# The router's column sums behind the first half of the output projection, the residual's factor on VectorE, the further blocks' slots two pairs later

## Chip, cores and metric

One core of one Trainium2 chip. The metric is device time in microseconds (us) of one execution of the program; lower is better.

## What is computed

One layer of a decoder for 512 tokens of width 1024, all in float32: a token mixer (attention, pooling and a state-space branch, merged and projected by `w_out`), a norm, a mixture of 32 experts, and a norm. What the change touches is the end of the first part and the start of the second. Cut from the reference:

```python
x = layer_norm(DN_ALPHA * x + mix, ln1_g, ln1_b)          # mix = merged @ w_out
p_grp = softmax(xf @ w_grp + b_grp); g_sel = argmax(p_grp)
logit_e = (xf @ w_exp + b_exp)                            # top 2 experts inside the group
h = silu(xb @ w_gate[e]) * (xb @ w_up[e]); y = h @ w_down[e]
x = layer_norm(DN_ALPHA * x + ffn, ln2_g, ln2_b)          # DN_ALPHA = 2 ** 0.25
```

## The kernel before

**Front part.** `out_proj` multiplies the merged activations (`mh`, `ml`: a high and a low part) by `w_out` (`whl`: the same split). Each product takes three matmuls (L70, L71, L72). The first 512 columns of `w_out` are done for all four tiles of 128 tokens at once: 4 chunks of `whl` x 2 row blocks x 4 tiles x 3 = 96 matmuls into banks `ps_mm` and `ps_s`. Then, tile by tile, the second 512 columns follow, with the transposes of the finished rows (L1055), the router's logits (L1065) and the norm. The norm's gain is folded into the router's weights by `router_consts`: it loads the weights `wr` on ScalarE's DMA queue, multiplies them on VectorE (L933, L934), adds them up per column (`wsum`, L936), spreads the sums over all partitions by one matmul against ones (L938), and reads the result into `nsg` and `br` (L940, L941), which only the logits need (L1068, L1069).

**Expert part.** `moe` takes the experts in pairs. A pair's token rows are gathered from DRAM by an indirect DMA on POOL's queue (`fetch`, L1335), transposed (L1342) and multiplied by an expert's gate and up weights (64 matmuls, L1355); `hidden` makes `th` on ScalarE and VectorE; `turn` transposes it (L1374) and ScalarE copies it to `hT` (L1375); `flush` runs the 16 down matmuls (L1387), whose bank `ps_o` ScalarE and VectorE empty into `y` (L1391, L1393). After each pair `combine` adds the rows into `acc` (L1408, L1409 on TensorE, L1418 on VectorE). All expert weights, 192 pieces of 1 MB, come through SP's DMA queue in one fixed order into a ring of buffers (L1439); a piece is issued when the buffer that it goes into has been read.

**Extras in the first pairs.** `residual(t, c)` loads a half of the first norm's gain and shift into `t` (L1088, on ScalarE's DMA queue), multiplies it by ALPHA on ScalarE (L1089), and applies it to `acc` by 8 VectorE operations (L1092, L1093); it is called at experts 1 and 2. `route_further` (VectorE only) works out where tokens go whose expert has more than 64 rows; `slots_everywhere` (8 transposes of `dd`, L1304, copied to `db`) and `further_slots` (per token tile and choice three VectorE operations that write `og` and `rwo`, L1321 to L1323, and a small matmul, L1324) turn it into tables. All of it stood at experts 1 and 2.

**The loop for further blocks.** Between pairs 7 and 8 stands a loop on the chip (L1558) with a count that is read from memory; for this input its body is not run. All five engines meet at its entry. Ahead of it SP has issued 13 pieces that only experts 16 to 18 need (`held`); the next piece is issued behind the loop. In the compiled order SP's branch into the loop carries waits on the completion of the loads that it has issued; the other engines' branches wait for the release of the common barrier.

Within an engine instructions run in the order of the compiled list; a scheduler makes that list, except where `keep_in_program_order` or `inorder` pins an instruction.

Of the kernel before, what the change touches and what calls it, by code (L numbers as in the profile page):

```python
# [8 lines left out]
F32 = mybir.dt.float32  # L9
# [5 lines left out]
OP = mybir.AluOpType  # L15
# [6 lines left out]
NT = 4  # L22
# [8 lines left out]
ALPHA = 2.0 ** 0.25  # L31
# [8 lines left out]
def dram(ap, offset, dims):  # L40
    return bass.AP(tensor=ap.tensor, offset=ap.offset + offset, ap=dims)


class Build:
# [869 lines left out]
    def router_consts(self, p):  # L914

        nc, I = self.nc, self.I
        V = nc.vector.tensor_tensor
        wr = p.tile([128, KD, 36], F32, name="wr")
        for i in range(2):
            ks = slice(i * 4, i * 4 + 4)  # L920
            nc.scalar.dma_start(wr[:, ks, 0:4], dram(I["router_w_grp"], i * 2048, [[16, 128], [4, 4], [1, 4]]))
            nc.scalar.dma_start(wr[:, ks, 4:36], dram(I["router_w_exp"], i * 16384, [[128, 128], [32, 4], [1, 32]]))
        br = p.tile([128, 36], F32, name="br")
        nc.scalar.dma_start(br[:, 0:4], dram(I["router_b_grp"], 0, [[0, 128], [1, 4]]))
        nc.scalar.dma_start(br[:, 4:36], dram(I["router_b_exp"], 0, [[0, 128], [1, 32]]))
        for i, nm in enumerate(("ln1_g", "ln1_b")):
            nc.scalar.dma_start(self.gb[:, i].rearrange("p (i k) -> p i k", i=2), dram(I[nm], 0, [[4, 128], [512, 2], [1, 4]]))
        ones = p.tile([128, KD, 128], F32, name="xT", bufs=2)[:, 0]
        nc.gpsimd.memset(ones, 1.0)
        bc = [128, KD, 36]  # L930
        wb = p.tile([128, KD, 128], F32, name="xT", bufs=2)[:, :, 0:36]
        sm = p.tile([128, 2, 36], F32, name="wsum")
        V(wb, wr, self.gb[:, 1, :, None].to_broadcast(bc), OP.mult)  # L933
        V(wr, wr, self.gb[:, 0, :, None].to_broadcast(bc), OP.mult)  # L934
        for i, t in enumerate((wr, wb)):
            nc.vector.tensor_reduce(sm[:, i], t.rearrange("p k n -> p n k"), axis=AX.X, op=OP.add)  # L936
        ps = self.bank("o")
        nc.tensor.matmul(ps[:, 0:72], ones, sm.rearrange("p i n -> p (i n)"), start=True, stop=True)  # L938
        nsg = p.tile([128, 36], F32, name="nsg")
        nc.vector.tensor_scalar(nsg, ps[:, 0:36], -1.0, None, op0=OP.mult)  # L940
        V(br, br, ps[:, 36:72], OP.add)  # L941
        return wr, nsg, br

    def out_proj(self, mh, ml):

        nc = self.nc
# [3 lines left out]
        for tt in range(NT):  # L950
# [2 lines left out]
            R.append(r)  # L953
        w = [[self.load_cols(I["w_out"], D, i * 512, 512, k0=4 * j, nk=4, t=self.rc.tile([128, 2048], F32, name="rc", bufs=4))
              for j in range(2)] for i in range(2)]
        rc = self.router_consts(p)

        def evac(half, tt, a):
            o = R[tt][:, half * 512:(half + 1) * 512]
            nc.vector.scalar_tensor_tensor(o, o, 2.0 * ALPHA, a, op0=OP.mult, op1=OP.add)  # L960
# [11 lines left out]
                 for k4 in range(4)]  # L972
        for tt in range(NT):
            evac(0, tt, accs[tt])

        rows = [self.bank("s") for _ in range(2)]
        lg = p.tile([128, NT, 36], F32, name="lg")
# [94 lines left out]
    def norm1_apply(self, p, tt, mv, rs):  # L1072
# [7 lines left out]
            nc.scalar.activation(r[:, c], r[:, c], AF.Identity, bias=nm, scale=rs)  # L1080
        nc.gpsimd.dma_start(self.zd[tt * 128:(tt + 1) * 128], r)

    def residual(self, t, c):

        nc = self.nc
        cs = slice(c * 512, (c + 1) * 512)
        for i, nm in enumerate(("ln1_g", "ln1_b")):
            nc.scalar.dma_start(t[:, i], dram(self.I[nm], c * 512, [[0, 128], [1, 512]]))  # L1088
        nc.scalar.mul(t, t, ALPHA)  # L1089
        for tt in range(NT):  # L1090
            r = self.acc[tt // 2][:, tt % 2, cs]
            self.tc.keep_in_program_order(nc.vector.tensor_tensor(r, r, t[:, 0], OP.mult))  # L1092
            nc.vector.tensor_tensor(r, r, t[:, 1], OP.add)  # L1093


    def first_max(self, p, v, rev, m, oh, name):
# [212 lines left out]
    def further_slots(self, part):  # L1309

        nc = self.nc
        T = nc.vector.tensor_scalar
        p = self.rt
        if part == 0:
            self.fps = self.bank("pt")[0:64, 0:32]
        for tt in (part * 2, part * 2 + 1):
            for i in range(2):
                rk = self.og0[:, tt % 2 * 2 + i, 0:64]
                wo = p.tile([128, 2, 16], F32, name="rwo", bufs=4)
                io, bk = self.io128[:, 0:16], self.blk[:, tt, i:i + 1]  # L1320
                T(rk, self.io64[:, 0:64], self.rr[:, tt, i:i + 1], None, op0=OP.is_equal)  # L1321
                T(wo[:, 0], io, bk, self.tok[:, tt:tt + 1], op0=OP.is_equal, op1=OP.mult)
                T(wo[:, 1], io, bk, self.wk[:, i, tt:tt + 1], op0=OP.is_equal, op1=OP.mult)  # L1323
                self.inorder(nc.tensor.matmul(self.fps, rk, wo.rearrange("p a n -> p (a n)"), start=(tt == 0 and i == 0),  # L1324
                                              stop=(tt == NT - 1 and i == 1)))
        if part:
            T(self.idxo, self.fps[:, 0:16], 4096.0, None, op0=OP.add)
            for h in range(2):
                T(self.wt48[h * 64:(h + 1) * 64, 32:48], self.fps[:, 16:32], 0.5, None, op0=OP.mult)


    def gather(self, xs, idx):
# [119 lines left out]
    def moe(self):  # L1452
        p = self.ep
        self.worder, self.wt = [], []
        for e in range(E + 1):
            gu = [(e, m, i) for m in (0, 1) for i in (0, 1)] if e < E else []
            dn = [(e - 1, 2, i) for i in (0, 1)] if e else []
            self.worder += dn + gu if e == 2 * LOOP else gu + dn
        spare = self.spare
        xs1, gb = spare[:, :D], spare[:, D:].rearrange("p (i n) -> p i n", i=2)  # L1460
        xq = self.xq0
        xs = self.xq0.rearrange("p k n -> p (k n)")
        self.db = p.tile([128, 2, S], I16, name="db")
        pairs = E // 2
        pend = None
        self.terms = []

        def fetch(j, xs=xs):
            if j < pairs:
                self.gather(xs, self.idx[:, j:j + 1])  # L1470

        for e in range(E):
            pr, odd = e // 2, e % 2
            if pr == LOOP and not odd:
                self.flush(pend, self.turn(pend[1]))
                self.combine()
                pend = None

                held = self.worder.index((e, 0, 0)) + len(self.ring) - 7
                self.load_until(held)  # L1480
                self.overflow()
                self.npiece = held
                xq = self.gather_turn(xs)
                fetch(pr + 1)
            hT = []
            gu = self.gate_up(xq[:, :, odd * 64:(odd + 1) * 64], self.pieces(e, 0), self.pieces(e, 1),
                              (lambda: hT.append(self.turn(pend[1]))) if pend and e > 1 else None)
            if e == 0:
                self.load_until(len(self.first))
                fetch(1, xs1)  # L1490
                self.slot_weights()
                pend = (0, self.hidden(gu, self.wt48[:, 0:1]), None)
                continue
            if e == 1:
                fetch(2)
                hT.append(self.turn(pend[1]))
            if e == 2:
                self.slots_everywhere()
                self.further_slots(0)
                pend = (*pend[:2], self.slot_rows(self.sid[:, 0:1]))  # L1500
            end = pr == pairs - 1
            if end and not odd:
                self.load_until(len(self.worder))
            th = self.hidden(gu, self.wt48[:, e:e + 1])
            if odd:
                if not end and pr + 1 != LOOP:

                    xq = self.gather_turn(xs if pr else xs1)
                    if pr:
                        fetch(pr + 2)  # L1510
                if self.terms:
                    self.combine()
                self.y = self.ytile(end)
            if pend:
                self.flush(pend, hT[0])
            if e == 1:
                srt = self.route_further()
            if e == 2:
                self.further_slots(1)
                srt.close()  # L1520
            if e in (1, 2):
                self.residual(gb, e - 1)
            if odd and pr:
                ot = self.slot_rows(self.sid[:, pr:pr + 1], t=self.moe_tile() if end else None)
            pend = (e, th, ot if odd and pr else None)
        self.ahead = [self.start_tile(tt) for tt in range(2)]
        self.flush(pend, self.turn(pend[1]))
        self.steady = False
        return self.terms
# [230 lines left out]
```

## Time and profile before

| | |
|---|---|
| median of 3 runs | 1097.99 us (1094.75 to 1098.54) |
| the profiled execution | 1097.79 us, of which 1096.1 us span from the first to the last instruction |
| mean granted TensorE clock | 0.962 of 2.4 GHz |
| busy time over the span | PE 999.9 us (91%), DVE 593.6 us (54%), ACT 317.0 us (29%), POOL 201.1 us (18%) |
| read from HBM | 254.40 MB, 236 GB/s over the span |

PE is TensorE, DVE VectorE, ACT ScalarE, POOL GpSimd, SP the engine whose queue issues the large loads; a q behind a name is that engine's sequencer or DMA queue. A time is counted from the span's start. Busy shares are means over stages with different limits, so the rows below are read stage by stage. Ends of matmuls are modelled: back-to-back matmuls overlap in the rows, and the distance of their starts is the pace.

### The profile page before, as it was taken

The page shows a single profiled execution, that of the slowest core. Times are in us where ns is not written, and L with a number is a line of the kernel's source. Part 1 is how long each engine was busy: PE and PEld are TensorE (multiplying, and loading weights), DVE is VectorE, ACT ScalarE, POOL GpSimd, SP SyncE. Part 2 cuts the span into 40 slices and gives each one's busy share as a digit, 9 for nine tenths or more (in the row PEclk, how much of TensorE's full clock was granted, in tenths as well). Part 3 has the DMA queues.
Part 4 walks back from the last instruction along what each step waited for, and adds up shares of the span by engine and source line. Part 5 has one row for each costly group of instructions (what it writes and reads, how often), then busy time and mean ns, then how long its engine had stood idle before and what let it go on. Part 6 is the DMA issues. An engine that isn't in the chain of part 4 may idle for free. (4 is left out here: it accounts for less than half of the span.)

```text
span 1096.1 us, 15867 instructions
## 1 busy us (share of the span) xinstructions
PE 999.9 (91%) x6189; PEld 698.7 (64%) x6189; DVE 593.6 (54%) x1427; ACT 317.0 (29%) x662; POOL 201.1 (18%) x179
## 2 busy tenths in 40 slices
PE   7969988999989999999698879999996999999994
PEld 6956676778778777888585455555552655555552
DVE  7992667474788784253255384444444244444436
ACT  4322222334556564232122121111110111111112
POOL 5410213334111223453112000000000000000003
PEclk9995999999999899999899989999998899999997
DMA  6701442225111112735415999999998999999992
GB/s 201 225 1 23 98 82 77 78 71 165 38 39 40 39 39 66 281 115 198 158 74 215 409 382 418 418 418 419 418 419 360 403 418 418 418 418 418 419 375 77
DMA packets 79821, 256.21 MB, mean 234 GB/s; under 512 B 16544, under 2 KB 43712, under 8 KB 55168
## 3 DMA queue, kind: packets, MB, share of 16 engines
q1 hardware_dynamic: 68064, 245.56, 57.4%
q10 hardware_dynamic: 8944, 3.59, 2.1%
q0 software_dynamic: 2736, 6.03, 1.5%
q8 instruction: 49, 0.80, 0.3%
q14 instruction: 28, 0.23, 0.1%
HBM read 254.40 MB, written 4.69 MB: 236 GB/s over the span
## 5 line engine op out<-in xcount | busy, mean ns | idle before, releaser
L1355 PE MATMUL ps_mm<-w,xq 128*64 128x256 f32 x1296 | 148.3, 381 | 0.0
L102 POOL TENSOR_TENSOR whl<-w,whl 128x1024 fp32r<-128x1024 f32 (+3 forms) x41 | 94.7, 2318 | 278.7 <-ACT whl L113 237.9
L1355 PEld LDWEIGHTS ps_mm<-w,xq 128*64 128x64 f32 x1296 | 91.2, 137 | 53.3 <-issue 8.6
L72 PE MATMUL ps_mm<-xh,whl 128*128 128x512 f32 x288 | 115.8, 402 | 0.0
L71 PE MATMUL ps_mm<-xl,whl 128*128 128x512 f32 x288 | 115.4, 401 | 0.0
L70 PE MATMUL ps_mm<-xh,whl 128*128 128x512 f32 x288 | 115.2, 400 | 0.0
L1365 DVE SCALAR_TENSOR_TENSOR th<-th,ps_mm 128x256 f32<-128x256 f32 x32 | 13.5, 421 | 161.2 <-ACT th L1364 161.2
L1393 DVE TENSOR_TENSOR y<-ps_o,y 64x512 fp32r<-64x512 f32 x60 | 41.3, 689 | 86.7 <-ACT y L1391 79.3
L1335 POOL DMA_INDIRECT xq<-zd,idx x14 | 14.0, 1003 | 389.8 <-PE ps_pt L1408 306.3
L1391 ACT CAST y<-ps_o 64x512 fp32r<-64x512 f32 x60 | 34.8, 579 | 141.7 <-issue 81.9
L1387 PE MATMUL ps_o<-w,hT 128*64 128x512 f32 x288 | 69.6, 608 | 0.0
L72 PEld LDWEIGHTS ps_mm<-xh,whl 128*128 128x128 f32 x288 | 54.7, 190 | 11.0 <-issue 0.8
L71 PEld LDWEIGHTS ps_mm<-xl,whl 128*128 128x128 f32 x288 | 54.8, 190 | 10.3
L70 PEld LDWEIGHTS ps_mm<-xh,whl 128*128 128x128 f32 x288 | 54.6, 189 | 10.4 <-issue 0.9
L113 ACT CAST whl<-w 128x1024 fp32r<-128x1024 f32 (+3 forms) x56 | 54.7, 989 | 13.5 <-PE ps_mm L72 13.4
L1355 PE MATMUL ps_mm<-rc,xq 128*64 128x256 f32 x384 | 46.8, 393 | 0.0
L1387 PEld LDWEIGHTS ps_o<-w,hT 128*64 128x64 f32 x288 | 21.4, 139 | 36.0 <-issue 33.0
L1364 ACT ACTIVATE th<-ps_mm 128x256 f32<-128x256 f32 x32 | 12.3, 383 | 104.8 <-PE ps_mm L1355 104.8
L1355 PE MATMUL ps_mm<-rd,xq 128*64 128x256 f32 x368 | 42.2, 381 | 0.0
L1355 PEld LDWEIGHTS ps_mm<-rc,xq 128*64 128x64 f32 x384 | 27.9, 142 | 17.6 <-issue 4.9
L1418 DVE TENSOR_TENSOR acc<-acc,ps_pt 128x512 f32<-128x512 f32 x60 | 38.4, 677 | 0.0
L1418 DVE TENSOR_TENSOR acc<-acc,ps_s 128x512 f32<-128x512 f32 x60 | 38.2, 677 | 0.0
(581 smaller groups left out, 2064.4 us busy)
## 6 DMA issues: line engine op xcount, KB each, us to landing
w<-in_moe_w_up_dram SPq DMA_DIRECT2D x43, 1024.0 KB, 19.9
w<-in_moe_w_gate_dram SPq DMA_DIRECT2D x38, 1024.0 KB, 20.3
w<-in_moe_w_down_dram SPq DMA_DIRECT2D x37, 1024.0 KB, 20.0
w<-in_w_in_dram SPq DMA_DIRECT2D x17, 1024.0 KB, 5.0
rc<-in_moe_w_down_dram SPq DMA_DIRECT2D x14, 1024.0 KB, 19.9
rc<-in_moe_w_gate_dram SPq DMA_DIRECT2D x14, 1024.0 KB, 19.9
rd<-in_moe_w_down_dram SPq DMA_DIRECT2D x13, 1024.0 KB, 20.5
rd<-in_moe_w_gate_dram SPq DMA_DIRECT2D x12, 1024.0 KB, 14.6
```

Source lines behind the costliest of these rows:

```text
L70: mm(ps, a[0], b[0], start=start, stop=False)
L71: mm(ps, a[0], b[1], start=False, stop=False)
L72: mm(ps, a[1], b[0], start=False, stop=stop)
L102: (V if eng == "dve" else P)(dst, src, h, OP.subtract)
L113: pin(self.nc.scalar.copy(hv[:, :, c:c + w], src))
L1335: self.nc.gpsimd.indirect_dma_start(xs[:n], None, self.zd[:, :], bass.IndirectOffsetOnAxis(ap=idx, axis=0), bounds_check=S - 1, oob_is_err ...
L1355: self.inorder(nc.tensor.matmul(gu[hh * 64:(hh + 1) * 64, part * 256:(part + 1) * 256], xe[:, k], w[k // 4][:, k % 4, hh * 256:(hh + 1) * ...
L1365: nc.vector.scalar_tensor_tensor(th, th, 1.0, gu[:, 0:256], op0=OP.add, op1=OP.mult)
L1387: self.inorder(nc.tensor.matmul(y[dh][dh * 64:(dh + 1) * 64], hT[:, q, hh * 64:(hh + 1) * 64], wd[f // 2][:, f % 2, dh * 512:(dh + 1) * 51 ...
L1391: nc.scalar.copy(part(yh, dh), y[dh][dh * 64:(dh + 1) * 64])
L1393: nc.vector.tensor_sub(part(yl, dh), y[dh][dh * 64:(dh + 1) * 64], part(yh, dh).bitcast(F32))
L1418: self.nc.vector.tensor_tensor(a, a, ps, OP.add)
```

## The change

1. The matmul of the column sums and its two readers are cut out of `router_consts` into a function `sums()`, which `out_proj` calls behind the first half's results; the matmul is pinned there.
2. `residual` no longer loads or scales: `gains(t, c)` loads the gain and shift on POOL's DMA queue, half 0 at expert 0, half 1 at expert 1 behind the use of half 0; the factor ALPHA goes into the 8 VectorE operations, which become `scalar_tensor_tensor`. ScalarE's two multiplies of 128x1024 go.
3. `residual(gb, 0)` now stands ahead of `route_further`; `slots_everywhere` goes behind expert 1's down matmuls; the two parts of `further_slots` go from expert 2 to experts 4 and 6, each with a bank of its own, joined by a copy and an add in `rfs`.

```diff
@@ router_consts
-        ps = self.bank("o")
-        nc.tensor.matmul(ps[:, 0:72], ones, sm.rearrange("p i n -> p (i n)"), start=True, stop=True)
         nsg = p.tile([128, 36], F32, name="nsg")
-        nc.vector.tensor_scalar(nsg, ps[:, 0:36], -1.0, None, op0=OP.mult)
-        V(br, br, ps[:, 36:72], OP.add)
-        return wr, nsg, br
+
+        def sums():
+            ps = self.bank("o")
+            self.tc.keep_in_program_order(nc.tensor.matmul(ps[:, 0:72], ones, sm.rearrange("p i n -> p (i n)"), start=True, stop=True))
+            nc.vector.tensor_scalar(nsg, ps[:, 0:36], -1.0, None, op0=OP.mult)
+            V(br, br, ps[:, 36:72], OP.add)
+        return (wr, nsg, br), sums
@@ out_proj
-        rc = self.router_consts(p)
+        rc, sums = self.router_consts(p)
...
         for tt in range(NT):
             evac(0, tt, accs[tt])
+        sums()
@@ residual
+    def gains(self, t, c):
+        nc = self.nc
+        for i, nm in enumerate(("ln1_g", "ln1_b")):
+            nc.gpsimd.dma_start(t[:, i], dram(self.I[nm], c * 512, [[0, 128], [1, 512]]))
...
-        for i, nm in enumerate(("ln1_g", "ln1_b")):
-            nc.scalar.dma_start(t[:, i], dram(self.I[nm], c * 512, [[0, 128], [1, 512]]))
-        nc.scalar.mul(t, t, ALPHA)
         for tt in range(NT):
             r = self.acc[tt // 2][:, tt % 2, cs]
-            self.tc.keep_in_program_order(nc.vector.tensor_tensor(r, r, t[:, 0], OP.mult))
-            nc.vector.tensor_tensor(r, r, t[:, 1], OP.add)
+            self.tc.keep_in_program_order(nc.vector.scalar_tensor_tensor(r, r, ALPHA, t[:, 0], op0=OP.mult, op1=OP.mult))
+            nc.vector.scalar_tensor_tensor(r, t[:, 1], ALPHA, r, op0=OP.mult, op1=OP.add)
@@ moe
                 self.slot_weights()
+                self.gains(gb, 0)
...
-            if e == 2:
-                self.slots_everywhere()
-                self.further_slots(0)
-                pend = (*pend[:2], self.slot_rows(self.sid[:, 0:1]))
+            if e in (4, 6):
+                self.further_slots(e // 2 - 2)
+                if e == 6:
+                    srt.close()
...
-            if e == 1:
-                srt = self.route_further()
             if e == 2:
-                self.further_slots(1)
-                srt.close()
+                self.slots_everywhere()
+                self.terms[0] = (self.slot_rows(self.sid[:, 0:1]), *self.terms[0][1:])
             if e in (1, 2):
                 self.residual(gb, e - 1)
+            if e == 1:
+                self.gains(gb, 1)
+                srt = self.route_further()
```

**Place 1: TensorE in the first half of the projection.** `ps_s` and `ps_mm` are the banks of the four token tiles; L938 before and L941 in the change are the matmul of the sums. Before, it stands in the second chunk, behind 43 of the half's 96 matmuls:

```order
L72 MATMUL ps_mm<-whl,ml_4702 128x512
L70 MATMUL ps_s<-whl,mh_4700 128x512
L938 MATMUL ps_o<-wsum,xT 128x72
L71 MATMUL ps_s<-whl,mh_4700 128x512
L72 MATMUL ps_s<-whl,ml_4702 128x512
```

In the change it stands behind all 96, ahead of the first transposes:

```order
L71 MATMUL ps_s<-whl,mh_4701 128x512
L72 MATMUL ps_s<-whl,ml_4703 128x512
L941 MATMUL ps_o<-wsum,xT 128x72
L1058 MATMUL ps_pt<-ident,acc 128x128 x4
L70 MATMUL ps_mm<-whl,mh_4700 128x512
```

It has moved past the 53 matmuls that stood behind it in this half; nothing else on TensorE changes places there.

**Place 2: TensorE at experts 1 to 3.** L1387 (change: L1397) are down matmuls, L1304 (L1310) the transposes of `dd`, L1324 the small slot matmuls. Before:

```order
L1374 MATMUL ps_pt<-ident,th 128x128 x2
L1355 MATMUL ps_mm<-w,xq 64x256 x16
L1304 MATMUL ps_pt<-ident,dd 128x128 x8
L1324 MATMUL ps_pt<-rwo,og 64x32 x4
L1387 MATMUL ps_o<-w,hT 64x512 x4
L1387 MATMUL ps_o<-rd,hT 64x512 x4
L1324 MATMUL ps_pt<-rwo,og 64x32 x4
L1355 MATMUL ps_mm<-rd,xq 64x256 x16
```

In the change:

```order
L1384 MATMUL ps_pt<-ident,th 128x128 x2
L1365 MATMUL ps_mm<-w,xq 64x256 x16
L1397 MATMUL ps_o<-w,hT 64x512 x4
L1397 MATMUL ps_o<-rd,hT 64x512 x4
L1310 MATMUL ps_pt<-ident,dd 128x128 x8
L1365 MATMUL ps_mm<-rd,xq 64x256 x16
```

The transposes of `dd` now follow expert 1's down matmuls, and the slot matmuls have left this stretch for the gate and up matmuls of experts 4 and 6.

**Place 3: POOL's queue at the start of the experts.** L1335 (change: L1345) are the gathers, L1036 (L1039) part of the router's weights. Before:

```order
L1335 DMA w<-zd,idx 128x1024
L1036 TENSOR_TENSOR w<-O,wt_5409 128x256 x3
L1335 DMA xq<-zd,idx 128x1024 x7
L1556 TENSOR_LOAD bi
```

In the change:

```order
L1345 DMA w<-zd,idx 128x1024
L1039 TENSOR_TENSOR w<-O,wt_5409 128x256 x3
L1090 DMA w<-in_ln_g_dram 128x512
L1090 DMA w<-in_ln_b_dram 128x512
L1345 DMA xq<-zd,idx 128x1024
L1090 DMA w<-in_ln_g_dram 128x512
L1090 DMA w<-in_ln_b_dram 128x512
L1345 DMA xq<-zd,idx 128x1024 x6
```

The four loads of gain and shift have come into POOL's queue, two ahead of the gather for pair 2 and two ahead of that for pair 3. SP's queue is the same in both, piece for piece.

## Rows read from the trace of the kernel before

**Rows 1.** Windows: busy time by engine in each stretch, granted clock, DMA share, GB/s.

```profile
605.00:610.00 5.00, 5.00 (x50) 3.30 (x48) 0.00 (x0) 0.00 (x0) 0.00 (x0) 1.00 1.01 363
640.00:645.00 5.00, 5.00 (x16) 2.45 (x13) 2.58 (x12) 0.00 (x0) 0.00 (x0) 0.62 0.88 311
645.00:650.00 5.00, 5.00 (x48) 4.28 (x47) 3.12 (x8) 2.47 (x4) 0.00 (x0) 1.00 1.00 361
650.00:655.00 5.00, 5.00 (x44) 3.51 (x38) 4.90 (x11) 1.04 (x4) 0.31 (x1) 1.00 0.95 383
654.00:820.00 166.00, 162.06 (x1122) 92.92 (x1122) 70.07 (x133) 31.60 (x71) 6.00 (x6) 1.00 1.01 419
842.00:852.00 10.00, 3.19 (x15) 2.23 (x16) 4.80 (x10) 0.52 (x2) 0.28 (x1) 0.66 0.57 211
```

**Rows 2.** Timeline of TensorE: start of pair 3 and of pair 4.

```profile
709.09 1.23 PE L1342 MATMUL ps_s<-ident,xq 128*128 128x128 f32 x8
736.92 1.23 PE L1342 MATMUL ps_s<-ident,xq 128*128 128x128 f32 x8
```

**Rows 3.** Timeline around the loop: last load ahead, first behind, first matmuls behind.

```profile
828.47 0.33 SPq L1439 DMA_DIRECT2D rc<-in_moe_w_up_dram  x1
849.00 0.34 SPq L1439 DMA_DIRECT2D w<-in_moe_w_up_dram  x1
849.46 1.98 PE L1342 MATMUL ps_s<-ident,xq 128*128 128x128 f32 x8 [6.81 <-issue]
```

**Rows 4.** SP's waits, 820 to 852 us (us in total, times, longest).

```profile
SPq L1558 <- DMA rc<-in_moe_w_up_dram: 2.4, 1, 2.4
```

**Rows 5.** Line 1558, the loop's entry: duration ns min/median/max, first and last start.

```profile
L1558 SPq EVENT_SEMAPHORE  x19: 17/28/28, 829.6 to 848.8; - x19
L1558 DVEq EVENT_SEMAPHORE  x13: 21/50/50, 844.2 to 849.0; - x13
```

**Rows 6.** DMA issues: KB each, median us from issue to landing.

```profile
rc<-in_moe_w_up_dram SPq DMA_DIRECT2D x10, 1024.0 KB, 19.9
w<-in_ln_b_dram ACTq DMA_DIRECT2D x2, 256.0 KB, 9.8
xq<-zd,idx POOLq DMA_INDIRECT x14, 8.2
```

**Rows 7.** Timeline near the end: expert 31's last up piece, issued and first used.

```profile
1035.97 0.33 SPq L1439 DMA_DIRECT2D rc<-in_moe_w_up_dram  x1
1056.22 1.90 PE L1355 MATMUL ps_mm<-rc,xq 128*64 128x256 f32 x16
```

**Rows 8.** Timeline of the first half of the projection.

```profile
519.17 0.39 PE L70 MATMUL ps_s<-whl,mh 128*128 128x512 f32 x1
...
524.62 0.39 PE L70 MATMUL ps_s<-whl,mh 128*128 128x512 f32 x1
531.14 0.46 DVE L933 TENSOR_TENSOR xT<-wr,gb 128x288 f32<-128x288 f32 x1 [7.85 <-DMA rc<-in_moe_w_down_dram]
...
534.34 0.67 PE L938 MATMUL ps_o<-wsum,xT 128*128 128x72 f32 x2 [9.34 <-DVE wsum L936]
...
548.43 0.63 PE L1055 MATMUL ps_pt<-ident,acc 128*128 128x128 f32 x4
```

**Rows 9.** SP's waits, 590 to 660 us (us in total, times, longest).

```profile
SPq L1439 <- PE ps_mm L1355: 23.1, 6, 16.4
```

**Rows 10.** Timeline of experts 0 to 2.

```profile
615.79 1.06 ACT L1089 ACTIVATE w<-w 128x1024 f32<-128x1024 f32 x1 [12.67 <-DMA w<-in_ln_b_dram]
...
617.16 5.02 PE L1387 MATMUL ps_o<-rc,hT 128*64 128x512 f32 x16 [5.32 <-ACT hT L1375]
...
635.91 0.27 PE L1324 MATMUL ps_pt<-rwo,og 128*64 128x32 f32 x2 [4.26 <-DVE rwo L1323]
```

**Rows 11.** Lines 1092 and 1400 on VectorE: duration ns min/median/max, first and last start.

```profile
L1092 DVE TENSOR_TENSOR acc<-acc,w x8: 672/682/691, 632.1 to 652.6; 128x512 f32<-128x512 f32 x8
...
L1400 DVE SCALAR_TENSOR_TENSOR ot<-db,sid,ot x15: 750/750/753, 639.7 to 1038.1; 128x512 fp32r<-128x512 int16 x15
```

More of the change, by code (lines that the diff above doesn't have):

```diff
@@ L1314, in further_slots @@
         if part == 0:
-            self.fps = self.bank("pt")[0:64, 0:32]
+            self.fsum = p.tile([64, 32], F32, name="rfs")
+        fps = self.bank("pt")[0:64, 0:32]
         for tt in (part * 2, part * 2 + 1):
@@ L1323, in further_slots @@
                 T(wo[:, 1], io, bk, self.wk[:, i, tt:tt + 1], op0=OP.is_equal, op1=OP.mult)
-                self.inorder(nc.tensor.matmul(self.fps, rk, wo.rearrange("p a n -> p (a n)"), start=(tt == 0 and i == 0),
-                                              stop=(tt == NT - 1 and i == 1)))
+                self.inorder(nc.tensor.matmul(fps, rk, wo.rearrange("p a n -> p (a n)"), start=(tt % 2 == 0 and i == 0),
+                                              stop=(tt % 2 == 1 and i == 1)))
         if part:
-            T(self.idxo, self.fps[:, 0:16], 4096.0, None, op0=OP.add)
+            nc.vector.tensor_tensor(self.fsum, self.fsum, fps, OP.add)
+            T(self.idxo, self.fsum[:, 0:16], 4096.0, None, op0=OP.add)
             for h in range(2):
-                T(self.wt48[h * 64:(h + 1) * 64, 32:48], self.fps[:, 16:32], 0.5, None, op0=OP.mult)
+                T(self.wt48[h * 64:(h + 1) * 64, 32:48], self.fsum[:, 16:32], 0.5, None, op0=OP.mult)
+        else:
+            nc.vector.tensor_copy(self.fsum, fps)
     def gather(self, xs, idx):
```

## The prediction

> **What bounds the kernel now.** I read the windows first, for the stream of expert weights. From 654 to 820 us the DMA share is 1.01 and the rate 419 GB/s, with TensorE busy 162.06 of 166 us [rows 1]: two things run near their limits, and the question is which of them sets the end. A pair's twelve pieces of 1 MB (12.58 million bytes) take 30.0 us at 419 GB/s; TensorE's pairs start 27.83 us apart [rows 2]. So TensorE is a little faster than the stream, and lives on the lead that the ring of buffers gives it. Does the lead last? The last up piece of expert 31 is issued at 1035.97 and lands a median of 19.9 us later [rows 6], at 1055.9; its first matmul starts at 1056.22 [rows 7]. It is 0.35 us in hand. At the end both limits meet: the kernel gets shorter only if TensorE and the stream both do.
>
> Then I looked for where the two are tied, and that is the loop's entry. SP issues its last piece ahead of it at 828.47 and the next at 849.00, and TensorE starts pair 8 at 849.46 after 6.81 us of idling [rows 3]. The compute engines are not what the entry waits for: VectorE, the last of them, reaches it at 844.2, SP's own semaphore events run on until 848.8 [rows 5]. SP stands there waiting for loads [rows 4], and the last piece, issued at 828.47, lands by the median at 848.4. So the entry is a **gate that opens when the stream has run dry**, and 4.6 us of lead on the compute side are thrown away there. Behind the gate both sides start anew from the same state, with 13 pieces in place and nothing under way, and from there to the end the change alters nothing.
>
> From this follows the rule for the whole sum: the end moves by what the gate moves, and the gate moves by what the **stream** moves, as long as the compute engines are there first.
>
> **What sets the stream's start.** SP's longest wait between 590 and 660 us, 16.4 us, is for gate matmuls [rows 9]: those of expert 0, which free the first buffer. It ends at some 597.5, and behind it comes the burst from which the stream is full. Up to there everything hangs on TensorE and the routing behind it, so microseconds of TensorE saved ahead of it move the stream one for one.
>
> **The change part by part.**
>
> *Sums behind the first half.* The 43rd matmul of the half starts at 524.62; then TensorE stands still until 534.34, for the sums of the router's weights (9.34 us put down to `wsum`), which VectorE could not begin before 531.14, when their loads were in [rows 8]. The transposes behind the half start at 548.43. Without the wait: 524.62 is 24 matmuls behind 519.17, so one takes 0.227 us at full clock; the 43rd is through at 524.85, and the 53 that follow take 12.0 us, to 536.9. The sums' matmul took 0.67 us behind the stall; at full pace I put it at 0.4. The transposes start at 537.3 instead of 548.43: **11.1 us earlier** (10.9 if the sums' matmul stays at 0.67). That is more than the stall, since the matmuls behind it ran slow: the clock granted in that stretch is part of the loss.
>
> Can a wait come back there? The sums are ready at 534.3 in either order, as nothing ahead of them on VectorE or in the loads changes; TensorE asks for them at 536.9. That is 2.6 us in hand. Behind L941 stand the transposes, behind `nsg` and `br` on VectorE the statistics of the next rows; none of them waits for more than this one matmul. I take 11.1. From here to the burst the order of every engine is as before, so the burst comes at 586.4.
>
> *ScalarE's multiplies and the moved extras.* ScalarE waits 12.67 us for the gain's loads at expert 0 and holds expert 0's `hT` behind its multiply; TensorE idles 5.32 us for that and runs its next sixteen matmuls in 5.02 us [rows 10]. The change takes this away. At expert 2 TensorE idles 4.26 us for the first of the slot tables [rows 10]; these go to experts 4 and 6, where the DVE operations have most of a pair's time to be ready. In place of them comes one wait: `residual(gb, 0)` is put ahead of `route_further`, 8 operations of 0.68 us (the old form) to 0.75 us (the nearest row with the new operation) [rows 11], 5.5 to 6.0 us, and TensorE needs its `dd` after expert 1's down matmuls. I let it cost all of 6.0. So TensorE and VectorE come out at least 5.3 + 4.3 - 6.0 = 3.6 us ahead here, at most 9.6, beyond the 11.1.
>
> By the rule above this is worth nothing at the end by itself. It is worth what it gives the stream. From 640 to 655 the rate drops to 311, 361 and 383 GB/s [rows 1], since pieces wait for buffers that the late matmuls have not freed. Against 419 this is (108 + 58 + 36) / 419 x 5 = 2.4 us of stream. With the matmuls earlier by more than the stream, buffers are free in time and the dip closes. But the second pair of gain loads, which now falls into the dip, will then take its share from a full stream. What that costs is seen where the first pair falls into one: 363 instead of 419 from 605 to 610 [rows 1], 0.7 us. The dip gives **1.7 us** (bounds: nothing, if something else makes it, and 2.4).
>
> *The gain loads on POOL's queue.* The same bytes, on another queue: two ahead of the gather for pair 2, two ahead of that for pair 3. The gathers on this queue land after 8.2 us, the loads on ScalarE's after 9.8 [rows 6]; the queue as such shows no penalty, and I cost the move at nothing. Behind the waiting VectorE stand `th`, the slots and `combine`'s adds, and TensorE waits for those; the lateness that this cover can take is worked out with the last rival.
>
> The Trainium skill speaks against this move: "SBUF — State Buffer", section "SBUF: two separate sides", says that loads issued from POOL get their descriptors from GpSimd, which VectorE locks out of a shared port while it runs certain fast copies, and recommends ScalarE's or SP's queue for such loads. The gathers' row does not agree as far as it goes, since they land early beside a busy VectorE. By the Trainium skill's rule the time would be that of the last rival below.
>
> *Ahead of the gate.* The compute side gains 14.7 to 20.7 us, the stream 11.1 + 1.7 = 12.8. The compute engines' lead at the gate, 4.6 us, becomes 6 to 12 us. Should they run into the stream ahead of it, they are still in time: the last piece that expert 15 needs is 13 pieces, 32 us, ahead of the one that opens the gate.
>
> **The sum**, against the profiled execution of 1097.8 us, whose median of three runs is 0.2 us higher: 1097.8 - 11.1 - 1.7 = 1085.0 us. With the bounds of the two terms it is 1084.3 to 1086.9; I give the likeliest case 1083.5 to 1086.
>
> **Rivals.**
>
> *The gate opens for the compute engines.* Were the wait at the loop not for the loads to land, it would open up to 20 us earlier, SP would not pause, and the dip around it (211 GB/s over 10 us from 842 to 852 [rows 1], 5.0 us of stream) would close as well: 1085.0 - 5.0 = 1080.0, and no less, because the last pieces then set the end [rows 7]. For it speaks that the barrier is common to five engines and SP is only one of them; against it, that SP's events end within 0.4 us of the last piece's landing.
>
> *Only the front counts.* The dip at 640 to 655 stays, if the gain loads and the gathers make it and not the buffers: 1086.7, or 1087.4 if the second pair of loads costs its 0.7 in addition. For it speaks that the first pair made a dip by itself in a full queue; against it, that SP waits for matmuls five more times before 660 us [rows 9] and that the dip is far deeper.
>
> *The change doesn't do what it says.* The wait for the sums comes back behind the half, if the router's loads land later than in this execution: each microsecond past the 2.6 in hand costs one. Land they 5 us later, the gain at the front is 8.7 and the time 1087.4; come they at the old 548, only the dip is left, 1096. I put 1088 to 1096 here.
>
> *Slower.* The gain loads land late, VectorE stands in `residual` with everything queued behind it, and TensorE follows. The gate hides the first 6 to 12 us of that, and the saving of 12.8 has to be eaten up as well: a hold of VectorE beyond some 19 to 25 us decides it, and one of 31 us, in the worse case, gives 1097.8 + 12 = 1110. Against it, the loads on the two queues land within 10 us in the median [rows 6]. By the Trainium skill's rule on loads from POOL's queue ("SBUF — State Buffer", "SBUF: two separate sides") this is the case that would come about.
>
> **Numbers.** Likeliest case 64 in 100, 1085.0 us. Only the front 18, the gate for the compute engines 8, the sums' wait back 5, slower 3; 2 for what I do not see. The range 1081 to 1089 holds the first two and part of the third case, the scatter of the runs included, and leaves out less than 2 in 10. A measurement of this kernel tells about 0.5% (5.5 us) from no change; below 1092.5 lie the first three cases and half of the fourth: faster 0.93, same 0.04, slower 0.03.
>
> **What would show it.** In the profile after: no idle time of TensorE put down to `wsum`, transposes of the first rows at about 537.3; SP's burst at about 586.4; 419 GB/s through what was 640 to 655; no wait of TensorE on `hT` at expert 0; at the loop SP's events ending at about 836 and TensorE idle there for well over 6.8 us; the stretch from pair 8's start to the end as long as before. It is wrong if SP passes the loop without waiting for its loads, if the burst does not move with the transposes, or if the end lies nearer than before to the gate, since then something behind the gate was not the same.

## The result and the profile after

The changed kernel takes 1082.26 us (median of 4 runs, 1081.56 to 1085.79) against 1097.71 us for the kernel before (4 runs): a ratio of 0.987, with a 95% interval of 0.9842 to 0.9899. The prediction was 1085.0 us, with a range of 1081 to 1089. In the profiled execution of after the span is 1081.1 us, 15.0 us shorter than before.

**The front.** Timeline of TensorE behind the first half (after; start, duration, engine and line):

```profile
535.56 0.34 PE L941 MATMUL ps_o<-wsum,xT 128*128 128x72 f32 x2
535.73 0.67 PE L1058 MATMUL ps_pt<-ident,acc 128*128 128x128 f32 x4
```

The wait of 9.34 us for `wsum` [rows 8] is gone, and the transposes start at 535.73 instead of 548.43. Of these 12.7 us 1.3 belong to neither part of the change: ScalarE issues the router's first weights (L921) at 515.29 before and at 514.00 after, and up to there the two programs are the same. Counted from that issue, SP's burst comes after 82.26 us before and after 70.88 after: the first part of the change gave **11.4 us**.

**The burst, the loop and the start of pair 8.** Timeline of SP's queue and of TensorE (after):

```profile
584.88 0.33 SPq L1449 DMA_DIRECT2D w<-in_moe_w_up_dram  x1
...
813.07 0.33 SPq L1449 DMA_DIRECT2D rc<-in_moe_w_up_dram  x1
833.96 0.34 SPq L1449 DMA_DIRECT2D w<-in_moe_w_up_dram  x1
...
834.24 1.98 PE L1352 MATMUL ps_s<-ident,xq 128*128 128x128 f32 x8 [20.32 <-DMA rc<-in_moe_w_up_dram]
```

SP's hole at the loop (from its last issue ahead of it to its first behind) is 20.9 us long, nearly as it was (20.5 [rows 3]), and what ended TensorE's idle time is named now: the landing of the last piece. TensorE stood there for 20.32 us instead of 6.81. Line 1570 (the loop's entry) shows who was late:

```profile
L1570 SPq EVENT_SEMAPHORE  x19: 17/28/28, 814.2 to 833.7; - x19
L1570 DVEq EVENT_SEMAPHORE  x13: 21/50/50, 815.5 to 833.9; - x13
```

VectorE was there at 815.5, 18.2 us ahead of SP's last event; before, these were 844.2 and 848.8 [rows 5]. From SP's first piece behind the loop to the end of the span it takes 247.1 us in both.

**The stream.** Windows of after (columns as in [rows 1]): the stretch that answers to 640 to 655 before, 12.7 us earlier; then one on each pair of gain loads.

```profile
627.00:642.00 15.00, 14.34 (x94) 7.81 (x94) 9.94 (x24) 2.46 (x6) 0.70 (x1) 1.00 1.02 419
...
595.00:598.00 3.00, 3.00 (x28) 1.88 (x25) 0.00 (x0) 0.00 (x0) 0.00 (x0) 1.00 1.03 321
611.00:619.00 8.00, 6.12 (x44) 3.57 (x42) 7.40 (x27) 2.33 (x4) 0.55 (x1) 1.00 1.02 414
```

The dip to 311, 361 and 383 GB/s [rows 1] has closed to 419. From the burst to the last piece ahead of the loop it is 228.2 us instead of 230.9: **2.7 us**, and 0.4 go again in the longer hole, so that the gate opens 2.4 us earlier, counted from the burst (249.08 instead of 251.45). The first pair of gain loads makes a dip of its own still (321 GB/s in 595 to 598, with the DMA share at 1.03: the engines are busy and move less); the second pair, issued at 610.3 and landed by 619.1, makes hardly any (414 over that time, some 0.1 us).

So the 15.0 us are 1.3 (the execution's own start) + 11.4 (front) + 2.7 (dip) - 0.4 (hole).

### The profile page after: what moved, and what is told of

Same layout as the page of the kernel before. It is cut to its first block, busy times and chain, and to the rows that moved or that the text cites. A ratio compares the mean times of both kernels' runs of the same rounds, so it can differ in the third digit from the quotient of the medians.

```text
span 1081.1 us, 15866 instructions
## 1 busy us (share of the span) xinstructions
PE 990.5 (92%) x6189; PEld 695.3 (64%) x6189; DVE 594.2 (55%) x1429; ACT 314.9 (29%) x660; POOL 204.0 (19%) x183
## 5 line engine op out<-in xcount | busy, mean ns | idle before, releaser
L102 POOL TENSOR_TENSOR whl<-w,whl 128x1024 fp32r<-128x1024 f32 (+3 forms) x41 | 95.1, 2329 | 276.6 <-ACT whl L113 238.5
L1345 POOL DMA_INDIRECT xq<-zd,idx x14 | 14.1, 1008 | 371.3 <-PE ps_pt L1418 264.8
L1397 PE MATMUL ps_o<-w,hT 128*64 128x512 f32 x288 | 67.9, 595 | 0.0
L1397 PEld LDWEIGHTS ps_o<-w,hT 128*64 128x64 f32 x288 | 21.3, 137 | 34.9 <-issue 31.9
L1385 ACT COPY hT<-ps_pt 128x256 f32<-128x256 f32 x32 | 11.9, 372 | 90.6 <-PE ps_pt L1384 90.6
## 6 DMA issues: line engine op xcount, KB each, us to landing
rc<-in_moe_w_gate_dram SPq DMA_DIRECT2D x14, 1024.0 KB, 20.5
```

Of the source, the lines that this page charges most:

```text
L102: (V if eng == "dve" else P)(dst, src, h, OP.subtract)
L1345: self.nc.gpsimd.indirect_dma_start(xs[:n], None, self.zd[:, :], bass.IndirectOffsetOnAxis(ap=idx, axis=0), bounds_check=S - 1, oob_is_err ...
L1397: self.inorder(nc.tensor.matmul(y[dh][dh * 64:(dh + 1) * 64], hT[:, q, hh * 64:(hh + 1) * 64], wd[f // 2][:, f % 2, dh * 512:(dh + 1) * 51 ...
```

## Experiments

All eleven are compared with the kernel before on the same chip. One table ahead of them, from SP's queue in each profile: from the issue of the router's weights (L921 on ScalarE's queue) to the burst; from the burst to the last piece ahead of the loop; the hole; from the first piece behind the loop to the end of the span.

| kernel | median, us | to the burst | burst to last piece | hole | to the end |
|---|---|---|---|---|---|
| before | 1097.71 | 82.26 | 230.9 | 20.5 | 247.1 |
| after | 1082.26 | 70.88 | 228.2 | 20.9 | 247.1 |
| after, again | 1082.05 | 70.89 | 228.0 | 20.9 | 247.1 |
| 1: sums alone | 1085.25 | 74.64 | 231.3 | 21.2 | 247.0 |
| 2: without the sums | 1093.04 | 82.61 | 228.1 | 20.9 | 247.1 |
| 3: slots at expert 2 | 1084.99 | 72.77 | 228.0 | 21.0 | 247.1 |
| 4: gain on ScalarE | 1084.59 | 72.98 | 229.6 | 20.5 | 246.8 |
| 5: matmuls ahead | 1085.65 | 74.61 | 228.6 | 23.5 | 247.2 |
| 6: matmuls behind | 1104.08 | 70.90 | 228.6 | 20.3 | 267.1 |
| 7: no loop | 1077.85 | 70.90 | 228.2 | none | none |
| 8: sums behind 72 | 1085.29 | 73.63 | 228.0 | 20.9 | 247.2 |
| 10: split on VectorE | 1085.05 | 71.97 | 228.1 | 20.8 | 247.2 |
| 11: gains later | 1081.35 | 72.46 | 227.7 | 20.8 | 247.3 |

The end is the sum of the four columns and of L921's own start. With the sums behind the half the way to the burst varies by up to 3.8 us, which the theory did not name and experiment 10 looks at. Apart from that a column moves by more than 1 us only where the edit puts a wait or work into it or takes one out. L921 itself starts between 512.7 and 515.5 us in these profiles, in code that no edit touches: that much, 2.8 us, two profiles differ by before anything of this study begins. Before's median beside the experiments was 1096.06 to 1096.26 us.

**1. The sums alone.** Before, with the first part of the diff and nothing else.

> Before, with the first part of the change alone. Theory (the stream sets the gate and the gate the end): the burst of SP comes as much earlier as the transposes behind the first half, 11.4 us; the dip of the stream behind it stays as it was, since TensorE and the stream move by the same amount; the end comes 11.4 us earlier, at 1086.3 us by the medians (1097.7 before). Rival (the stalls of TensorE at experts 0 to 2 count at the end by themselves, 5.3 + 4.3 us): of the 15.4 us that the whole change gave only 5.8 are left for the sums, and the time is 1091.9 us.

1085.25 us against 1096.06, ratio 0.9892 [0.9878, 0.9906]: the theory's time by the medians. TensorE still stands for `hT` and for the slot tables (its timeline), and the dip is there in full and more, some 46 us behind the burst as before (windows):

```profile
606.68 6.33 PE L1390 MATMUL ps_o<-rc,hT 128*64 128x512 f32 x16 [5.02 <-ACT hT L1378]
626.74 0.39 PE L1327 MATMUL ps_pt<-rwo,og 128*64 128x32 f32 x2 [4.26 <-DVE rwo L1326]
```

```profile
631.00:633.00 2.00, 2.00 (x8) 1.10 (x6) 2.00 (x11) 0.00 (x0) 0.00 (x0) 0.50 0.98 381
633.00:635.00 2.00, 2.00 (x7) 1.05 (x5) 0.41 (x3) 0.00 (x0) 0.00 (x0) 0.50 0.19 70
635.00:637.00 2.00, 2.00 (x15) 0.95 (x12) 0.00 (x0) 1.22 (x2) 0.00 (x0) 0.75 0.95 299
```

The stalls of 9 us stay and cost what they take from the stream: the gate opens 252.4 us behind the burst (before 251.45, after 249.08), and nothing more is lost behind it. The front gave 7.6 us in this profile, not 11.4, and its execution was the slowest of the four (1088.50 us); experiment 10 goes into that.

**2. Without the sums.** The changed kernel, with the sums' matmul where it stood.

> The change without its first part: the sums' matmul stands in the second chunk again. Theory: the wait of 9.3 us for the sums is back; the stalls on hT and on the slot tables are gone, and the compute engines reach the loop some 14 us earlier than before; at the end only the closed dip of the stream is left of that, 2.4 us: 1095.3 us. Rival: the stalls count by themselves, 9.6 us or more: 1088.1 us or less.

1093.04 us, ratio 0.9975 [0.9966, 0.9985], 1.6 to 3.7 us less than before: the dip's 2.4, not the 9.6 of the stalls. TensorE waits for the sums again (first row), has no stall for `hT` or the slot tables, and most of what it wins stands at the loop (second row):

```profile
535.15 0.67 PE L938 MATMUL ps_o<-wsum,xT 128*128 128x72 f32 x2 [9.91 <-DVE wsum L936]
...
847.45 1.98 PE L1349 MATMUL ps_s<-ident,xq 128*128 128x128 f32 x8 [18.55 <-DMA rc<-in_moe_w_up_dram]
```

18.55 us of idling instead of 6.81, for an end that comes 1.9 us earlier in the profiles.

**3. Slot tables back at expert 2, and 4. gain and shift back on ScalarE.** Each takes one of the two other parts out of the change. In 3:

```diff
-            if e in (4, 6):
-                self.further_slots(e // 2 - 2)
...
+            if e == 2:
+                self.slots_everywhere()
+                self.further_slots(0)
```

> The change without its third part: the slot tables and the order of the residual as before. Theory: no wait for hT at expert 0, but the wait for the slot tables at expert 2 is back; the compute engines still reach the loop ahead of the last load, so the end moves only by what comes back of the dip, between 0 and 2.4 us: 1082.3 to 1084.7 us, and the rate of the stream some 45 us behind the burst tells how much. Rival: the stall counts by itself, 4.3 us and the slow matmuls behind it: 1086.6 us or more.

In 4 `residual` loads on ScalarE's queue and multiplies there, as before, ahead of `route_further`.

> The change without its second part: gain and shift are loaded on ScalarE's queue at the residual's place and multiplied by ScalarE. Theory: hT of expert 0 and the residual are late again by 5 us or more, the routing of the further tokens stands behind the residual and is late as well, and TensorE idles for hT and dd; the end moves only by the dip that this makes, 0 to 2.4 us: 1082.3 to 1084.7 us, as long as the compute engines reach the loop ahead of the last load (18 us in hand in the changed kernel). Rival: the stall counts by itself, 5.3 us or more: 1087.6 us or more.

1084.99 us (ratio 0.9888 [0.9872, 0.9904]) and 1084.59 us (0.9884 [0.9869, 0.9899]): neither loses what its stall costs TensorE. 3 lies 0.3 us above its expected range; its way to the burst is 1.9 us longer than after's, which the expectation did not have in it. The columns say what the medians cannot resolve: without the third part the dip closes all the same (228.0), without the second it closes by half (229.6). In these profiles the second part is enough for the dip, and the third adds nothing to the end. TensorE's start of pair 8, first in 3 and then in 4:

```profile
834.85 1.98 PE L1348 MATMUL ps_s<-ident,xq 128*128 128x128 f32 x8 [11.98 <-DMA rc<-in_moe_w_up_dram]
```

```profile
838.56 1.98 PE L1349 MATMUL ps_s<-ident,xq 128*128 128x128 f32 x8 [6.26 <-issue]
```

By these idle times the third part is worth 8 us of TensorE's lead at the loop and the second 14, and nearly all of it is thrown away there.

**5 and 6. The same work on TensorE ahead of the loop and behind it.**

```diff
+                t = self.bank("pt")
+                for _ in range(96):
+                    self.tc.keep_in_program_order(self.nc.tensor.matmul(t[:, 0:128], self.ident, self.ident, start=True, stop=True))
```

> The changed kernel with 96 more matmuls of 128x128 on TensorE, the identity with itself, behind pair 7 and ahead of the loop; their result is read by nothing. Worked out from eight transposes of that size in about 1.0 us: 12 us of work. Theory (the entry opens when the last load has landed): TensorE reaches the entry 12 us later, still ahead of the landing; the idle time there goes from 20.3 to about 8 us, and the end stays at 1082 us. Rival (the entry opens for the compute engines): the end comes 12 us later, 1094 us.

> The changed kernel with the same 96 matmuls behind the loop, between the transposes of pair 8 and its first gate matmuls. Theory: behind the entry TensorE runs without a pause to the end, so the same work costs its whole length there: 12 us, 1094 us; a little more if its first matmuls run at the lower clock and the weight pieces do not make it up. Rival (the stream sets the end behind the loop, with TensorE in hand): less than 12 us, and nothing if TensorE had 12 us in hand: 1082 to 1090 us.

The work was sized wrong: each matmul of the identity counts twice in the trace, and the 96 took 21.7 and 22.2 us instead of 12. The eight matmuls of `dd` against the identity would have told it: 16 records in 2.02 us in after. TensorE around the loop, first in 5 and then in 6:

```profile
817.68 21.68 PE L1489 MATMUL ps_pt<-ident 128*128 128x128 f32 x192
841.50 1.23 PE L1352 MATMUL ps_s<-ident,xq 128*128 128x128 f32 x8 [2.14 <-DVE ot L1410]
```

```profile
834.86 1.98 PE L1352 MATMUL ps_s<-ident,xq 128*128 128x128 f32 x8 [20.12 <-DMA rc<-in_moe_w_up_dram]
836.64 22.18 PE L1497 MATMUL ps_pt<-ident 128*128 128x128 f32 x192
```

So the test came out harsher than meant, and tells more. Behind the loop 22 us of work cost 20.0 (267.1 instead of 247.1); the time is 1104.08 us, ratio 1.0074 [1.0051, 1.0096]. There TensorE sets the pace: in after it waits for no load from 850 to 1050 us, and in 6 it is SP that waits, for buffers that TensorE has not read. The only wait of TensorE in that stretch of after and the longest of SP in 6 (us in total, times, longest):

```profile
PE ps_s L1418 <- ACT xq L1252: 3.9, 6, 0.7
```

```profile
SPq L1449 <- PE ps_mm L1365: 48.3, 22, 22.6
```

Ahead of the loop the same work ended at 839.4. By the usual hole of 20.9 the entry would have opened at 837.0; SP's first piece came at 839.68, so the hole grew by 2.6 us, and that is all that 21.7 us of work cost. The lead at the loop is a real cover and it is some 19 us deep. The entry opens for whichever side comes last: for the loads in after, and for TensorE as soon as it is later. Line 1573, the entry in 5, shows it: TensorE comes at 839.4, and one of SP's semaphore events lasts 4.12 us:

```profile
L1573 SPq EVENT_SEMAPHORE  x19: 17/28/4122, 817.3 to 837.9; - x19
L1573 PEldq EVENT_SEMAPHORE  x13: 51/51/51, 839.4 to 841.1; - x13
```

The median is 1085.65 us, ratio 0.9894 [0.9872, 0.9915]; besides the 2.6 us of the hole the way to the burst was 3.7 us longer in this profile, for the reason that experiment 10 looks at.

**7. No loop.** The call of the loop for further blocks is taken out.

> The changed kernel without the loop for further blocks (left out: the body, which does not run for this input, and the meeting of all engines at its entry). Theory: the stream no longer runs dry there, which gives back the hole of about 5 us (20.9 us between two issues against some 16 at 2.5 us a piece); TensorE does not stand for 20 us but catches up with the stream and waits for pieces later, so the end gains only what the stream gains: 1077 us. Rival (the compute engines set the end, and the gate threw away their lead): up to 18 us less, 1064 us.

1077.85 us, ratio 0.9828 [0.9805, 0.9851]: 4.2 us under the changed kernel (as run again in experiment 9) by the medians, 3.9 from the burst to the end of the span (492.4 instead of 496.2). The 18 us of lead do not come out. The waits of TensorE from 800 to 1045 us show why (us in total, times, longest):

```profile
PE ps_mm L1365 <- DMA w<-in_moe_w_gate_dram: 3.4, 7, 0.6
PE ps_mm L1365 <- DMA rc<-in_moe_w_gate_dram: 1.7, 3, 0.6
PE ps_mm L1365 <- DMA w<-in_moe_w_up_dram: 1.6, 3, 0.6
```

With the pause gone TensorE catches up with the stream, the first time at 873 us, and from then on waits half a microsecond at one piece after the other. The loop's price here is 3.9 us of the stream's pause and not TensorE's 18 us of lead; without the loop the stream sets the end.

**8. The sums behind 72 matmuls.** `sums()` is called in the third of the half's four chunks.

> The changed kernel with the sums' matmul behind 72 of the half's 96 matmuls instead of behind all. Theory: TensorE asks for the sums 5.4 us earlier, at about 530; VectorE has them at 532.5 to 534.8, so a wait of 2.4 to 4.7 us comes back, and the matmuls behind it may run slow for some us; all of it shifts the burst and so the end: 1085 to 1088 us. Rival (a wait of a few us there is absorbed before the burst or at the loop): 1082.3 us.

1085.29 us, ratio 0.9911 [0.9881, 0.9941], an interval that overlaps after's; the profile tells the two apart. The wait is back, and it is paid:

```profile
531.62 0.41 PE L941 MATMUL ps_o<-wsum,xT 128*128 128x72 f32 x2 [2.43 <-DVE wsum L936]
```

The way to the burst is 73.63 us, 2.7 more than after, and from the burst to the end it is 496.2 us in both. A microsecond ahead of the burst is a microsecond at the end; at experts 0 to 2 it was not.

**9. The changed kernel again.**

> The changed kernel once more, for its own scatter. Theory: the burst of SP comes 71 to 73 us behind the issue of the router's first weights on ScalarE's queue, by whether VectorE's operations ahead of the sums run beside POOL's share of the split; from the burst to the last load ahead of the loop 228 us, the hole 20.9, from the entry to the end 247.1 us; 1082 us.

1082.05 us, ratio 0.9864 [0.9841, 0.9887], and the same four columns to 0.2 us.

**10. The second quarter of the split on VectorE.** In five of the profiles with the sums behind the half the way to the burst was 72.5 to 74.6 us instead of 70.9, and in all five VectorE's product of the router's weights takes 2.65 us, elsewhere 0.45. It stands beside a share of the split that POOL does. Experiment 11 shows it; VectorE, POOL, TensorE:

```profile
531.58 2.65 DVE L934 TENSOR_TENSOR wr<-wr,gb 128x288 f32<-128x288 f32 x1
...
531.41 2.51 POOL L102 TENSOR_TENSOR whl<-rc,whl 128x1024 fp32r<-128x1024 f32 x1 [6.32 <-ACT whl L113]
...
537.19 0.74 PE L1058 MATMUL ps_pt<-ident,acc 128*128 128x128 f32 x4 [1.23 <-DVE acc L962]
```

VectorE's operation starts 0.17 us behind POOL's and ends 0.3 us behind POOL's end (534.2 and 533.9); the rest of VectorE's queue shifts by 2.2 us, and TensorE's transposes wait 1.23 us for `acc`. In after the product starts first and takes 0.45 us, and the next share of the split on VectorE (L102) takes 2.44 us instead of 1.22; a reduction (L936, one input) beside the same share of POOL's is not held:

```profile
530.97 0.45 DVE L934 TENSOR_TENSOR wr<-wr,gb 128x288 f32<-128x288 f32 x1
...
531.91 0.67 DVE L936 TENSOR_REDUCE wsum<-wr 128x36 f32<-128x288 f32 x1
532.50 2.44 DVE L102 TENSOR_TENSOR whl<-rc,whl 128x1024 fp32r<-128x1024 f32 x1
...
531.46 2.40 POOL L102 TENSOR_TENSOR whl<-rc,whl 128x1024 fp32r<-128x1024 f32 x1 [6.42 <-ACT whl L113]
```

Which of the two starts first decides it in all eleven profiles in which the sums stand later than before: in the five POOL's share begins 0.2 to 0.8 us ahead of the product, in the other six 0.4 to 1.1 us behind it. The experiment takes POOL's share away at that place:

```diff
-        ... eng=("dve", "pool")[k4 % 2])
+        ... eng=("dve", "dve", "dve", "pool")[k4])
```

> The changed kernel with the second quarter of the second columns' split on VectorE instead of POOL (behind the sums on VectorE). Theory: no operation of VectorE ahead of the sums runs beside one of POOL, so the product of the router's weights takes 0.45 us instead of the 2.65 of most runs, the sums are in time for TensorE and the transposes follow them without a wait; against a run of the changed kernel in which they waited the end comes 1 to 2 us earlier, against the one that did not the same: 1080.5 to 1082.5 us. Rival (the long products have another cause than POOL's operation beside them): they stay long, and the time as well.

1085.05 us, ratio 0.9895 [0.9875, 0.9914]: no gain, and if anything a loss (the intervals overlap). L934 takes 0.45 us and the sums are in time, as expected, but the collision has only moved. VectorE and POOL:

```profile
532.94 3.97 DVE L102 TENSOR_TENSOR whl<-rc,whl 128x1024 fp32r<-128x1024 f32 x2
...
532.29 2.39 POOL L102 TENSOR_TENSOR whl<-rc,whl 128x1024 fp32r<-128x1024 f32 x1 [13.56 <-ACT whl L113]
```

POOL's other share has come forward, and two operations of 1.22 us take 3.97 beside it; the transposes wait 0.83 us, and the way to the burst is 71.97. That VectorE is held by POOL stands by both forms of it; the step of the expectation that fell is that nothing else of POOL would take the place. The Trainium skill, "SBUF — State Buffer", section "SBUF: two separate sides", states the rule that fits: a pair of ports is shared by VectorE and GpSimd under an exclusive lock, taken for a whole instruction by whichever starts first, where VectorE reads two operands from SBUF and GpSimd reads SBUF too. The trace agrees: 2.65 us instead of 0.45 for the one that starts second, with its end 0.3 us behind POOL's.

**11. The first gain loads later**, behind the gather for pair 2 on POOL's queue (issued at 601.1 instead of 591.0).

> The changed kernel with the first pair of gain loads behind the gather for pair 2 on POOL's queue instead of ahead of it, some 9 us later. Theory: they land at about 608 us, VectorE stands in the residual for some 3 us and the compute engines reach the loop later by that; the end stays at 1082 us. The rate of the stream tells what makes its dip 10 us behind the burst: if the gain loads, the dip comes 9 us later; if it stays at its place, they do not make it. Rival (a hold of VectorE in the residual is paid at the end): 1085 us.

1081.35 us, ratio 0.9857 [0.9835, 0.9878]. VectorE stands 4.40 us for the gain, and the routing behind it is late, so TensorE idles 7.80 us instead of 1.88 for `dd`; the loop swallows it (timelines of VectorE and TensorE):

```profile
611.33 0.69 DVE L1098 SCALAR_TENSOR_TENSOR acc<-acc,w 128x512 f32<-128x512 f32 x1 [4.40 <-DMA w<-in_ln_g_dram]
...
623.01 3.75 PE L1310 MATMUL ps_pt<-ident,dd 128*128 128x128 f32 x16 [7.80 <-DVE dd L1264]
835.22 1.98 PE L1352 MATMUL ps_s<-ident,xq 128*128 128x128 f32 x8 [11.63 <-DMA rc<-in_moe_w_up_dram]
```

And the short dip of the stream has moved with the loads: there is none 10 us behind the burst, and one behind the later issue (windows):

```profile
596.00:599.00 3.00, 3.00 (x32) 1.91 (x28) 0.00 (x0) 0.00 (x0) 0.00 (x0) 1.00 1.03 426
608.00:611.00 3.00, 3.00 (x30) 1.96 (x30) 0.00 (x0) 0.37 (x1) 0.00 (x0) 1.00 0.96 336
```

It is the first pair of gain loads that makes it. The expected 3 us of standing were 4.4 and the rival's 1085 did not come.

## Why the prediction was right

**The rule.** "The end moves by what the gate moves, and the gate moves by what the stream moves, as long as the compute engines are there first" is what the runs show: 246.8 to 247.3 us behind the entry in every kernel that keeps the loop and changes nothing behind it; 9 us of TensorE's stalls kept ahead of it cost 3.3 us, all of it in the stream (experiment 1), 22 us of work added there cost 2.6 (5), and of 22 us added behind it 20 are paid (6).

**The front, 11.1 us.** It measured 11.4 from the issue of the router's weights, where no wait came back. But the reason given for the cover was wrong. The prediction said that the sums are ready at the same time in either order, "as nothing ahead of them on VectorE or in the loads changes", 2.6 us ahead of TensorE's asking. What changes is POOL beside VectorE: with TensorE's stall gone, POOL's next share of the split runs beside the sums. Where it holds the product, the sums come up to 0.5 us late, `acc` is late by 1.23 us, and in two of the five profiles TensorE's clock was down in the microseconds behind that (0.84 and 0.85 over 530 to 540). The front then gives 7.6 to 9.8 us. The rival of the returning wait was thus half alive, by another way than the late load that it named, and at 1.6 to 3.8 us. That the profile of after shows the whole 11.4 is in part luck: of the nine profiles with the sums behind the half and POOL's share in its place, four show it and five do not.

**The dip, 1.7 us.** Mis-sized: it measured 2.7 to the last piece and 2.4 to the opening of the gate, which is the upper bound. The 0.7 us that were taken off for the second pair of gain loads did not come. The first pair does cost some 0.7 us (321 of 419 GB/s for 3 us), and experiment 11 shows that it is the loads; the second pair, of the same size and on the same queue, passes at 414. Why is open.

**The lead at the gate, 6 to 12 us.** It was 18. The prediction added up idle times (5.3 and 4.3 us, less 6.0 for the residual) and left out a second wait for the slot tables, of 2.00 us, and the matmuls at the lower clock behind each wait, as in 640 to 645 before (0.62 [rows 1]); and the residual ahead of the routing cost a wait of 1.88 us for `dd`, not 6. TensorE, first before and then after:

```profile
638.18 1.43 PE L1324 MATMUL ps_pt<-rwo,og 128*64 128x32 f32 x5 [2.00 <-DVE rwo L1323]
```

```profile
615.56 2.02 PE L1310 MATMUL ps_pt<-ident,dd 128*128 128x128 f32 x16 [1.88 <-DVE dd L1264]
```

These terms were not taken apart by a run of their own. Nothing of this reaches the end, so the error was free, but a larger lead is also a larger cover: what can be late there is 18 us, not 12.

**The rivals.** The gate that opens for the compute engines: out, by the 20.32 us that TensorE stands there in after and by 5 and 6. Its price of 5.0 us for the pause was a little high, by 7 it is 3.9. Only the front: out, since the dip closed. Slower by late gain loads: they landed after 6.3 to 8.6 us on POOL's queue (7.8 to 11.8 on ScalarE's before), in time for VectorE at 605.3, and even 4.4 us of lateness cost nothing. The rule of the Trainium skill that spoke against the move ("SBUF — State Buffer", "SBUF: two separate sides": loads from POOL's queue get no descriptors while VectorE runs certain fast copies) did not show itself here: the second pair landed after 6.3 and 8.0 us while VectorE was busy for 7.40 of 8 us (611 to 619). Whether any of VectorE's operations there were of that kind no run shows.

**The sum.** 11.1 + 1.7 = 12.8 were forecast, 15.0 measured between the two profiles. Of the difference of 2.2 us 1.3 is the execution's own start, 0.3 the front and 1.0 the dip, less 0.4 in the hole. The median fell by 15.4.

## What to carry to other kernels

Where two resources run near their limits, look for the places at which they are tied, and ask of each microsecond saved on which side of the tie it lies: here the first part of the change gave some four fifths of the gain, and two stalls of TensorE that look as large in the profile gave only what they took from the stream. A cover worked out on one engine's queue holds only if the neighbours that share something with it do not move; taking a stall away moves them. And a place at which every engine meets and all loads must land, costs the pause of the stream and hides what the compute engines lose ahead of it, here up to some 19 us.

## What the runs showed of the hardware that was not expected

An operation of VectorE on two tensors that started beside a running one of POOL's ended only with it or later: 0.45 us became 2.65 in five profiles, and 1.22 became 2.44 in the changed kernel's. Two loads of 256 KB took 0.7 us out of a full stream the first time (321 of 419 GB/s for 3 us) and some 0.1 us the second (414 for 8 us). A float32 matmul of 128x128 takes 0.23 us here (96 in 21.68) and stands in the trace as two records, where a transpose of that size is one record and eight take 1.23 us.
